# Last round of an MLP reordered, weight offsets of the squares moved, norm rows issued earlier

## The chip, the cores and the metric

The kernel runs on one core of a Trainium2 chip. The metric is the device time of one execution in microseconds (us); of several runs the median is taken, and lower is better.

## The reference

One decoder layer on 256 tokens of width 2048, all in float32:

```python
h = rms_norm(x, norm1_g); proj = h @ w_in            # q/k/v of two head groups, forget logits
y_a = fox_attention(...)                             # 8 heads, causal with forget gates
y_b = dilated_attention(...)                         # 8 heads, three dilation patterns
x = x + concat(rms_norm(y_a), rms_norm(y_b)) @ w_out
h = rms_norm(x, norm2_g)
x = x + square(relu(h @ w_mlp_in)) @ w_mlp_out       # 2048 -> 8192 -> 2048
return rms_norm(x, final_norm_g)
```

## The kernel before

**Products.** Every float32 product is made of three matmuls. Each operand is split into an upper part (rounded to the format that TensorE takes, by ScalarE) and the rest (VectorE): `whi`, `wlo` for weights, `aT_hi`, `aT_lo` for activations; upper x upper, upper x lower and lower x upper are added up in PSUM. So TensorE needs, for each 256 rows of a weight chunk (a step), one ScalarE pass and one VectorE pass over the raw weights, which SP's queue loads a megabyte at a time into four `raw` tiles.

**Chunks and steps.** A chunk is 512 columns of a weight matrix. The 12 projection chunks and 8 output chunks come first, then the MLP in four rounds r of 2048 hidden units: four up chunks u(r, c) and four down chunks d(r, c). A chunk of the MLP has 8 steps of two rows (128 inputs each). In the up chunks (`turned_product`, L414) the weights are loaded into the array and the 256 tokens are streamed: 12 matmuls of 256 columns a row, upper weights twice, then lower, for each 128 columns. In the plain down chunks (`product`, L397 to L399) the squared activations are loaded and 512 weight columns are streamed.

**Seven-product chunks.** Seven of the sixteen down chunks, d(r, 1) and d(0..2, 0), use seven block products in place of eight (`seven_products`, L457). Their sums need sums of activations, `mix_hi` and `mix_lo`, made after each up chunk from the squares, and sums of weights (`both`, made by VectorE). They come in units of four steps (near, first, odd, even), woven into other chunks by `mixed`: d(r, 0) into the up chunks of the next round, d(r, 1) together with the plain d(r, 2). They hold the four PSUM banks `sc`, `sc`, `tr`, `tr`; plain chunks use the four `acc` banks. `drain_seven` empties the four banks into `xs` in four parts after the chunk's last unit, on VectorE, with two copies by ScalarE.

**Order.** It is written out by hand in `steps`. A round is: four up chunks (with the d of the round before woven in), then the plain d(r, 3), then the pair of d(r, 1) and d(r, 2). The last round leaves d(3, 3) for the end, so there it is: up chunks with d(2, 0) woven in, the pair, the plain d(3, 0), and d(3, 3) in `last_chunk`. Beside each row of a step, `run_side` issues what was put there with `at(slot, ...)`; there are two slots a step. All engines work in program order, so what stands behind a waiting instruction on its engine waits too.

**End.** `last_chunk` goes through the first 128 tokens at full width, then the other 128 tokens in two halves of 256 columns, so that `finish` (norm, gain, scaling, output DMAs) of the first runs under the products of the second. The final gain row `gf`, 1 MB spread over all partitions, is loaded by `load_gf` on SP's queue once the `late` pool is given up, whose place in memory it takes; `copies` of `drain_seven` lies in that pool. `put_gain` multiplies a 512-column piece by it on VectorE.

**Offsets.** Tiles are laid out so that operands start at chosen offsets within lines of 64 elements (256 bytes): `NEAR` = 8, `HIGH` = 24, `LOW` = 56, `MIX_HI` = 24, `MIX_LO` = 24 + 32. The pool `wide` starts with an 8-element tile `ahead`, so `aT_hi`, `aT_lo`, `big_hi` and `big_lo`, each 4096 elements a partition, all start at 8. `big_hi` and `big_lo` hold the attention's output first and then, in all four rounds, the squares. Weights of up chunks lie at 24 (upper) and 56 (lower); those of down chunks, which are streamed, at 8.

**Norm rows.** Near the start, `first_norm_rows` (slot 22) makes a diagonal of the norm factors on VectorE (L579), one matmul that spreads it over the partitions (L580), and a copy by ScalarE, which the drains of q and k chunks use.

Of the kernel before, what the change touches and what calls it, by code (L numbers as in the profile page):

```python
# [11 lines left out]
F32 = mybir.dt.float32  # L12
# [7 lines left out]
P = 128  # L20
# [4 lines left out]
NH = 8  # L25
# [16 lines left out]

LINE, NEAR, HIGH, LOW, GATED = 64, 8, 24, 56, 48
MIX_HI, MIX_LO = 24, 32
TURNED = "qku"
WARM, WARM2 = 8, 3

# [27 lines left out]
def kernel(  # L75
# [32 lines left out]
    dram = ctx.enter_context(tc.tile_pool(name="dram", bufs=1, space=DRAM))  # L108
    attention = ExitStack()
    mix = attention.enter_context(tc.tile_pool(name="mix", bufs=1))  # L110
    mix.tile([P, 40], F32, name="mix_begin")
    ctx.enter_context(tc.manual_schedule())


# [33 lines left out]
    for r in range(ROUNDS):  # L148
        for c in range(4):
            mine = plain(index["u", (r, c)])  # L150
            steps += mine[:4] + (mixed(index["d", (r - 1, 0)], c, mine[4:]) if r else mine[4:])
        late = [index["d", (r, c)] for c in range(4)]
        if r < ROUNDS - 1:
            steps += plain(late[3])
        for unit in range(4):
            steps += mixed(late[1], unit, plain(late[2])[2 * unit:2 * unit + 2])
        if r == ROUNDS - 1:
            steps += plain(late[0]) + plain(late[3])

    last_slot = {chunks[ci][:2]: 2 * i + 1 for i, (ci, _, _) in enumerate(steps)}  # L160
    units = list(dict.fromkeys((ci, s // 2) for ci, s, _ in steps))
# [224 lines left out]
    def operands(what, key):  # L386
        if what == "o":
            return yT_hi, yT_lo, key[0] * NH
        if what == "d":
            return hT_hi, hT_lo, 0  # L390
        return aT_hi, aT_lo, 0

    def product(acc, a, kt, t, w, j, cols, go, end):

        (ah, al, base), (hi, lo) = a, w
        xh, xl = (p[:, base + kt, t * P:(t + 1) * P] for p in (ah, al))
        nc.tensor.matmul(acc, xh, hi[:, j, cols], start=go, stop=False, skip_group_check=True)  # L397
        nc.tensor.matmul(acc, xl, hi[:, j, cols], start=False, stop=False, skip_group_check=True)  # L398
        nc.tensor.matmul(acc, xh, lo[:, j, cols], start=False, stop=end, skip_group_check=True)  # L399

    def turned_product(ci, i, j, kt, kts):

# [15 lines left out]
    def products(i, j):  # L418
        ci, s, sub = steps[i]
        what, key, _, _, _, cols, kts = chunks[ci]  # L420
        if sub:
            return seven_products(i, j)
        kt = 2 * s + j
        if what in TURNED:
            return turned_product(ci, i, j, kt, kts)
        a = operands(what, key)
        if cols > CW:
            return gated_products(ci, i, j, kt, kts, a)
        if kt == 0:
            accs[ci] = [psum.tile([P, CW], F32, name="acc", bufs=4) for _ in range(TB)]  # L430
        go, end = kt == 0, kt == kts - 1
        for t in range(TB):
            product(accs[ci][t], a, kt, t, splits[i], j, slice(0, CW), go, end)

    def seven_products(i, j):

        ci, s, sub = steps[i]
        if ci not in accs:
            accs[ci] = [psum.tile([P, CW], F32, name=n) for n in ("sc", "sc", "tr", "tr")]
        one_, two_, three, four = accs[ci]  # L440
        half, k1, k2 = CW // 2, 2 * s + j, 2 * s + 2 + j
        lower, upper = slice(0, P), slice(P, SEQ)
        h, m = (hT_hi, hT_lo), (mix_hi, mix_lo)
        todo = {
            "near": ((one_, 0, h, k2, lower), (one_, half, m, k2, lower)),
            "first": ((three, 0, h, k1, lower),),
            "odd": ((two_, half, m, k2, upper), (four, 0, m, k1, upper)),
            "even": ((three, half, m, k1, lower), (two_, 0, h, k2, upper)),
        }[sub]
        begin = j == 0 and s == 0  # L450
        hi, lo = splits[i]
        for n, (bank, c0, (ah, al), k, tokens) in enumerate(todo):
            acc = bank[:, c0:c0 + half]
            fresh = begin and (bank, sub) in ((one_, "near"), (three, "first"), (two_, "odd"), (four, "odd")) and (
                bank is not one_ or n == 0)
            for x, (a, w) in enumerate(((ah, hi), (al, hi), (ah, lo))):
                nc.tensor.matmul(acc, a[:, k, tokens], w[:, j, n * half:(n + 1) * half], start=fresh and x == 0,  # L457
                                 stop=s == KT // 2 - 2 and j == 1 and x == 2, skip_group_check=True)

# [89 lines left out]


    qkv = {}
    yT_hi = wide.tile([P, 2 * NH, SEQ], F32R, name="big_hi")
    yT_lo = wide.tile([P, 2 * NH, SEQ], F32R, name="big_lo")

    def drain_v(g, ci):
        acc = accs.pop(ci)
# [13 lines left out]

    rows1 = mix.tile([P, SEQ], F32, name="rows1")

    def first_norm_rows():
        d = two.tile([P, CW], F32, name="nat")
        square = d[:, SEQ:SEQ + P]
        nc.gpsimd.memset(square, 1.0)
        p = psum.tile([P, 512], F32, name="tr")
        for t in range(TB):
            nc.vector.tensor_scalar(d[:, t * P:(t + 1) * P], ident, rstd1[:, t:t + 1], None, op0=ALU.mult)  # L579
        nc.tensor.matmul(p[:, :SEQ], square, d[:, :SEQ], start=True, stop=True)  # L580
        nc.scalar.activation(rows1, p[:, :SEQ], AF.Copy)

# [133 lines left out]
        rsqrt(rstd2, ssq2s, D_MODEL)  # L716
        nc.vector.tensor_tensor(rstd2sq, rstd2, rstd2, op=ALU.mult)

    hT_hi, hT_lo = yT_hi, yT_lo

    def drain_u(c, ci):


        acc = accs.pop(ci)
        kept[c] = []
        for half in range(2):
            h = two.tile([P, CW], F32, name="nat")
            nc.scalar.activation(h, acc[half], AF.Relu)
            nc.scalar.activation(h, h, AF.Square)
            k0 = 4 * c + 2 * half  # L730
            split_psum(
                hT_hi[:, k0:k0 + 2, :].rearrange("p k s -> p (k s)"),
                hT_lo[:, k0:k0 + 2, :].rearrange("p k s -> p (k s)"), h,
            )
            kept[c].append(h.rearrange("p (k s) -> p k s", k=2))
# [64 lines left out]
    def square_and_gain(t, cs, n):  # L800
        unused = two.tile([P, CW], F32, name="nat")
        nc.scalar.activation(unused[:, :cs.stop - cs.start], xs[:, t, cs], AF.Square, accum_out=ssq3[:, t, n:n + 1])
        if n not in (1, 2):
            put_gain(t, cs)

    def add_down(acc, t, cs, n):
# [65 lines left out]
    for ci, (what, key, *_rest) in enumerate(chunks[:-1]):  # L872
        e = last_slot[what, key]
        if what == "v":
            at(e, drain_v, key, ci)
            if key == 0:
                at(e + 2, forget_gates)
                at(e + 6, gate_sums)
                at(e + 4, rel_row)
                at(e + 5, rel_back)  # L880
                at(e + 55, rel_turn)
        elif what in "qk":
            for half in range(2):
                late = half if what == "k" else (2 if key else 8) + 5 * half
                at(e + late, drain_qk, key, what, ci, half)
            if what == "k":
                kind = groups[key][4]
                for h in range(4):
                    n = e + 6 + 7 * (h // 2)
                    if kind == 0:  # L890
                        at(n - 3, decay_of, groups[key][3] * 4 + h)
                    at(n, scores, key, h)
                for h in range(4):
                    at(e + 20 + 7 * (h // 2), values, key, h)
                for h in range(4):
                    at(e + 13 + 7 * (h // 2), turn_probs, key, h)
                if key % 2:
                    at(e + 33, group_norm, kind)
        elif what == "o":
            at(e, drain_o, *key, ci)  # L900
            if key[0] == 1:
                for n in range(2):
                    at(e + 2, to_features, 4 * key[1] + 2 * n, 16)
                if key[1] == 3:
                    at(e + 4, second_norm)
        elif what == "u":
            at(e, drain_u, key[1], ci)
            at(e + 2, mix_activations, key[1])
            at(e + 4, split_mixed, key[1])
        elif ci in seven:  # L910
            for part in range(4):
                at(e + 1 + 2 * part, drain_seven, *key, ci, part)
            if key[0] == ROUNDS - 1:
                at(e + 7, load_gf)
                for c in (1, 2):
                    for t in range(TB):
                        at(e + 11 + 2 * c + t, put_gain, t, slice(c * CW, (c + 1) * CW))
        else:
            at(e, drain_d, *key, ci)

# [95 lines left out]
```

## Time and profile before

| what | value |
|---|---|
| median of 3 runs | 1099.67 us (1099.06 to 1099.78) |
| the profiled execution | 1097.77 us, span 1096.0 us |
| PE busy | 1080.1 us, 99% of the span |
| VectorE (DVE) busy | 800.7 us, 73% |
| ScalarE (ACT) busy | 604.1 us, 55% |
| DMA | 209.27 MB, 191 GB/s on average |
| mean granted TensorE clock | 0.996 |

PE is TensorE's matmuls, PEld its weight loads, POOL is GpSimd, and SPq the DMA issues of SyncE. Matmuls are pipelined, so the time that one costs is the distance between starts, or a group's time in the chain divided by its count; the duration of a single record is longer. The chain is the work that ended last, followed back from the end: at each step what released it, or what stood before it on its engine. A row of a group or of the timeline gives start, duration, engine, line, operation, result<-inputs, shapes and count, and in brackets the idle time before it with what ended it. A row of the waits reads: who <- for whom: us in total, times, longest. A row of DMA issues ends with the size of one and the median time from issue to landing.

### The profile page before, as it was taken

Reading aid. Unit: us, or ns where it says so; the run is one execution under the profiler, and the core shown is the slowest. Engines: PE = TensorE matmul, PEld = TensorE weight load, DVE = VectorE, ACT = ScalarE, POOL = GpSimd, SP = SyncE. Lnnn points to the kernel's source line nnn. Section 1 sums busy time; section 2 is a strip of 40 time slices with the busy share of each in tenths; the row PEclk is TensorE's granted clock in tenths of the full one; section 3 lists DMA queues with packets and bytes.
Section 4 is the critical chain, followed back from the end, with each engine's and each line's share of the span. In section 5 each row is a group of like instructions: output and inputs, shape, how many; then the busy total and the mean of one; then the engine's idle time right before and its main releaser. Section 6 shows DMA issues by size and latency. Waiting matters only on the chain.

```text
span 1096.0 us, 19064 instructions
## 1 busy us (share of the span) xinstructions
PE 1080.1 (99%) x7877; PEld 1014.8 (93%) x7877; DVE 800.7 (73%) x1076; ACT 604.1 (55%) x821; POOL 27.9 (3%) x42
## 2 busy tenths in 40 slices
PE   9999999999999999999999999999999999998996
PEld 7999899998988899998999998999998899998886
DVE  6666756667576666578777789787778887779774
ACT  6455545546455565655546665546666556666541
POOL 0010200000001000000000000000000000000000
PEclk9999999999999999999999999999999999999999
DMA  8665464655545567646766554675665666655642
GB/s 319 235 217 169 155 200 146 193 177 170 193 154 192 165 188 224 193 158 207 216 196 199 205 203 158 206 218 187 197 212 173 194 197 186 193 196 180 215 178 77
DMA packets 105395, 209.27 MB, mean 191 GB/s; under 512 B 3971, under 2 KB 5084, under 8 KB 105180
## 3 DMA queue, kind: packets, MB, share of 16 engines
q1 hardware_dynamic: 104412, 206.59, 57.7%
q8 instruction: 61, 1.00, 0.4%
q0 software_dynamic: 304, 1.06, 0.3%
q10 hardware_dynamic: 592, 0.40, 0.1%
q14 instruction: 26, 0.21, 0.1%
HBM read 205.93 MB, written 2.11 MB: 190 GB/s over the span
## 4 chain that ended last, share of the span: by engine, by line
PE 98%; ACT 0%; DVE 0%; DMA 0%; issue 0%; POOL 0%; ACTq 0%; DVEq 0%
PE acc L414 48%; PE acc L397 11%; PE acc L398 11%; PE acc L399 11%; PE sc L457 7%; PE tr L457 5%; PE tr L349 1%; PE sc L676 1%; PE sc L632 1%; PE tr L660 0%; DMA xs<-in_x_dram 0%; PE sc L628 0%; ACT whi L252 0%; PE sc L678 0%; PE sc L398 0%
## 5 line engine op out<-in xcount | busy, mean ns | idle before, releaser
L253 DVE TENSOR_TENSOR wlo<-raw,whi 128x1024 fp32r<-128x1024 f32 (+2 forms) x327 | 394.5, 1221 | 162.0 <-ACT whi L252 161.1
L252 ACT ACTIVATE whi<-raw 128x1024 fp32r<-128x1024 f32 (+2 forms) x328 | 339.2, 1050 | 228.3 <-PE acc L414 129.9
L414 PE MATMUL acc<-aT_hi,whi 128*128 128x256 f32 x1536 | 425.6, 277 | 0.0
L414 PE MATMUL acc<-aT_hi,wlo 128*128 128x256 f32 x1536 | 424.1, 276 | 0.0
L414 PE MATMUL acc<-aT_lo,whi 128*128 128x256 f32 x1536 | 423.9, 276 | 0.0
L414 PEld LDWEIGHTS acc<-aT_hi,whi 128*128 128x128 f32 x1536 | 288.1, 188 | 1.2 <-issue 0.9
L414 PEld LDWEIGHTS acc<-aT_lo,whi 128*128 128x128 f32 x1536 | 288.2, 188 | 0.3
L414 PEld LDWEIGHTS acc<-aT_hi,wlo 128*128 128x128 f32 x1536 | 288.1, 188 | 0.1
L397 PE MATMUL acc<-whi,big_hi 128*128 128x512 f32 (+1 forms) x414 | 160.2, 387 | 0.0
L398 PE MATMUL acc<-whi,big_lo 128*128 128x512 f32 (+1 forms) x414 | 159.9, 386 | 0.0
L399 PE MATMUL acc<-wlo,big_hi 128*128 128x512 f32 (+1 forms) x414 | 159.8, 386 | 0.0
L399 PEld LDWEIGHTS acc<-wlo,big_hi 128*128 128x128 f32 x414 | 78.1, 189 | 15.8
L398 PEld LDWEIGHTS acc<-whi,big_lo 128*128 128x128 f32 x414 | 78.1, 189 | 14.4
L397 PEld LDWEIGHTS acc<-whi,big_hi 128*128 128x128 f32 x414 | 78.1, 189 | 14.2
L218 ACT ACTIVATE whi<-both 128x1024 fp32r<-128x1024 f32 x56 | 59.7, 1066 | 49.0 <-DVE both L223 17.1
L219 DVE TENSOR_TENSOR wlo<-both,whi 128x1024 fp32r<-128x1024 f32 x56 | 68.3, 1220 | 4.7 <-ACT whi L218 3.8
L336 DVE TENSOR_TENSOR big_lo<-nat,big_hi 128x512 fp32r<-128x512 f32 x32 | 22.1, 692 | 42.3 <-ACT big_hi L335 42.3
L397 PE MATMUL acc<-whi,aT_hi 128*128 128x512 f32 (+1 forms) x144 | 51.7, 359 | 0.0
L398 PE MATMUL acc<-whi,aT_lo 128*128 128x512 f32 (+1 forms) x144 | 51.0, 354 | 0.0
L399 PE MATMUL acc<-wlo,aT_hi 128*128 128x512 f32 (+1 forms) x144 | 51.0, 354 | 0.0
L218 ACT ACTIVATE whi<-raw 128x1024 fp32r<-128x1024 f32 x28 | 29.6, 1056 | 11.6 <-PE sc L457 5.0
L335 ACT ACTIVATE mix_hi<-nat 128x512 fp32r<-128x512 f32 x32 | 18.5, 625 | 29.9 <-DVE nat L745 29.9
(212 smaller groups left out, 1359.5 us busy)
## 6 DMA issues: line engine op xcount, KB each, us to landing
raw<-in_w_mlp_in_dram SPq DMA_DIRECT2D x64, 1024.0 KB, 5.6
raw<-in_w_mlp_out_dram SPq DMA_DIRECT2D x64, 1024.0 KB, 5.1
raw<-in_w_in_dram SPq DMA_DIRECT2D x42, 1024.0 KB, 5.2
raw<-in_w_out_dram SPq DMA_DIRECT2D x16, 1024.0 KB, 5.1
raw<-in_w_in_dram SPq DMA_DIRECT2D x4, 1040.0 KB, 9.5
xs<-in_x_dram SPq DMA_DIRECT2D x3, 512.0 KB, 9.5
raw<-in_w_in_dram SPq DMA_DIRECT2D x2, 512.0 KB, 5.3
big_lo<-rel_d POOLq DMA_DIRECT2D x1, 1024.0 KB, 7.1
```

The costliest lines, as they stand in the source:

```text
L218: nc.scalar.activation(hi, src, AF.Copy)
L219: nc.vector.tensor_tensor(lo, src, hi.bitcast(F32), op=ALU.subtract)
L252: nc.scalar.activation(hi[:, :, c:c + step], t[:, :, c:c + step], AF.Copy)
L253: nc.vector.tensor_tensor(lo, t, hi.bitcast(F32), op=ALU.subtract)
L335: nc.scalar.activation(hi, src, AF.Copy)
L336: nc.vector.tensor_tensor(lo, src, hi.bitcast(F32), op=ALU.subtract)
L349: nc.tensor.transpose(p[:, j * SEQ + t * P:j * SEQ + (t + 1) * P], xs[:, t, c:c + P], ident)
L397: nc.tensor.matmul(acc, xh, hi[:, j, cols], start=go, stop=False, skip_group_check=True)
L398: nc.tensor.matmul(acc, xl, hi[:, j, cols], start=False, stop=False, skip_group_check=True)
L399: nc.tensor.matmul(acc, xh, lo[:, j, cols], start=False, stop=end, skip_group_check=True)
L414: nc.tensor.matmul(acc, w[:, j, b * P:(b + 1) * P], a[:, kt, :], start=kt == 0 and b % 2 == 0 and n == 0, stop=kt == kts - 1 and n == 2, s ...
L457: nc.tensor.matmul(acc, a[:, k, tokens], w[:, j, n * half:(n + 1) * half], start=fresh and x == 0, stop=s == KT // 2 - 2 and j == 1 and x ...
```

## The change

1. In the last round the plain chunk d(3, 0) moves ahead of the pair d(3, 1) and d(3, 2). The pair is then followed by `last_chunk`. The gain products of chunks 0, 1 and 2 are all issued at the end of the last chunk's first pass, chunk 0's too, which came with its squares before.
2. The three matmuls of a seven-product term come as upper x upper, upper x lower, lower x upper, so that the squares' upper part is loaded twice in a row (`seven_products`).
3. `big_lo` and `big_hi` change places and get 48 and 32 elements more. In rounds 0 and 1 the squares lie at 24 (upper) and 56 (lower) within the lines, in rounds 2 and 3 at 8 as before, as the attention's output does. The plain down chunks of rounds 0 and 1 also load the upper part twice in a row.
4. The diagonal of `first_norm_rows` is made at slot 19 by a function of its own; the matmul and the copy stay at slot 22.
5. Two pads shrink from 40 to 24 elements, which keeps the other pools' offsets.

```diff
+BIG_HI, BIG_LO, SHIFTED = 32, 48, 2
...
-    mix.tile([P, 40], F32, name="mix_begin")
+    mix.tile([P, 24], F32, name="mix_begin")
...
-        if r < ROUNDS - 1:
-            steps += plain(late[3])
+        steps += plain(late[3 if r < ROUNDS - 1 else 0])
         for unit in range(4):
             steps += mixed(late[1], unit, plain(late[2])[2 * unit:2 * unit + 2])
         if r == ROUNDS - 1:
-            steps += plain(late[0]) + plain(late[3])
+            steps += plain(late[3])
...
         if what == "d":
-            return hT_hi, hT_lo, 0
+            return *squares_of(key[0]), 0
...
-    def product(acc, a, kt, t, w, j, cols, go, end):
+    def product(acc, a, kt, t, w, j, cols, go, end, turn=False):
...
         nc.tensor.matmul(acc, xh, hi[:, j, cols], start=go, stop=False, skip_group_check=True)
-        nc.tensor.matmul(acc, xl, hi[:, j, cols], start=False, stop=False, skip_group_check=True)
-        nc.tensor.matmul(acc, xh, lo[:, j, cols], start=False, stop=end, skip_group_check=True)
+        rest = ((xl, hi), (xh, lo))
+        for n, (x, part) in enumerate(rest[::-1] if turn else rest):
+            nc.tensor.matmul(acc, x, part[:, j, cols], start=False, stop=end and n == 1, skip_group_check=True)
...
-            product(accs[ci][t], a, kt, t, splits[i], j, slice(0, CW), go, end)
+            product(accs[ci][t], a, kt, t, splits[i], j, slice(0, CW), go, end, what == "d" and key[0] < SHIFTED)
...
-            for x, (a, w) in enumerate(((ah, hi), (al, hi), (ah, lo))):
+            for x, (a, w) in enumerate(((ah, hi), (ah, lo), (al, hi))):
...
-    yT_hi = wide.tile([P, 2 * NH, SEQ], F32R, name="big_hi")
-    yT_lo = wide.tile([P, 2 * NH, SEQ], F32R, name="big_lo")
+    big_lo = wide.tile([P, KT * SEQ + BIG_LO], F32R, name="big_lo")
+    big_hi = wide.tile([P, KT * SEQ + BIG_HI], F32R, name="big_hi")
+
+    def rows_at(big, at):
+        return big[:, at:at + KT * SEQ].rearrange("p (k s) -> p k s", k=KT)
+
+    yT_hi, yT_lo = rows_at(big_hi, BIG_HI - 16), rows_at(big_lo, 0)
...
+    def first_norm_diagonal():
         d = two.tile([P, CW], F32, name="nat")
-        square = d[:, SEQ:SEQ + P]
-        nc.gpsimd.memset(square, 1.0)
-        p = psum.tile([P, 512], F32, name="tr")
+        diagonal.append(d)
+        nc.gpsimd.memset(d[:, SEQ:SEQ + P], 1.0)
         for t in range(TB):
             nc.vector.tensor_scalar(d[:, t * P:(t + 1) * P], ident, rstd1[:, t:t + 1], None, op0=ALU.mult)
...
+    def squares_of(r):
+        return (rows_at(big_hi, BIG_HI), rows_at(big_lo, BIG_LO)) if r < SHIFTED else (yT_hi, yT_lo)
...
-        if n not in (1, 2):
+        if n > 2:
             put_gain(t, cs)
...
                 at(e + 7, load_gf)
-                for c in (1, 2):
+                for c in range(3):
                     for t in range(TB):
-                        at(e + 11 + 2 * c + t, put_gain, t, slice(c * CW, (c + 1) * CW))
+                        at(e + 16 + c, put_gain, t, slice(c * CW, (c + 1) * CW))
...
+    at(19, first_norm_diagonal)
     at(22, first_norm_rows)
...
-            late5.tile([P, 40], F32R, name="late_begin")
+            late5.tile([P, 24], F32R, name="late_begin")
```

More of the change, by code (lines that the diff above doesn't have):

```diff
@@ L442, in seven_products @@
         lower, upper = slice(0, P), slice(P, SEQ)
-        h, m = (hT_hi, hT_lo), (mix_hi, mix_lo)
+        h, m = squares_of(chunks[ci][1][0]), (mix_hi, mix_lo)
         todo = {
@@ L571, with first_norm_rows @@
     rows1 = mix.tile([P, SEQ], F32, name="rows1")
-    def first_norm_rows():
+    diagonal = []
+    def first_norm_diagonal():
         d = two.tile([P, CW], F32, name="nat")
-        square = d[:, SEQ:SEQ + P]
-        nc.gpsimd.memset(square, 1.0)
-        p = psum.tile([P, 512], F32, name="tr")
+        diagonal.append(d)
+        nc.gpsimd.memset(d[:, SEQ:SEQ + P], 1.0)
         for t in range(TB):
             nc.vector.tensor_scalar(d[:, t * P:(t + 1) * P], ident, rstd1[:, t:t + 1], None, op0=ALU.mult)
+    def first_norm_rows():
+        d = diagonal.pop()
+        square = d[:, SEQ:SEQ + P]
+        p = psum.tile([P, 512], F32, name="tr")
         nc.tensor.matmul(p[:, :SEQ], square, d[:, :SEQ], start=True, stop=True)
@@ L717, in second_norm, with drain_u @@
         nc.vector.tensor_tensor(rstd2sq, rstd2, rstd2, op=ALU.mult)
-    hT_hi, hT_lo = yT_hi, yT_lo
-    def drain_u(c, ci):
+    def squares_of(r):
+        return (rows_at(big_hi, BIG_HI), rows_at(big_lo, BIG_LO)) if r < SHIFTED else (yT_hi, yT_lo)
+    def drain_u(r, c, ci):
+        hT_hi, hT_lo = squares_of(r)
         acc = accs.pop(ci)
@@ L906 @@
         elif what == "u":
-            at(e, drain_u, key[1], ci)
+            at(e, drain_u, *key, ci)
             at(e + 2, mix_activations, key[1])
```

## The prediction

> **What bounds the kernel now.** I read the engine line and the chain's shares first, then the chain piece by piece around the down projections, then the waits, then the timeline of VectorE and of the queue SP at the two places where TensorE stands still, and at the end.
>
> ```profile
> span 1096.0 us, 19064 instructions
> PE 1080.1 (99%) x7877; PEld 1014.8 (93%) x7877; DVE 800.7 (73%) x1076; ACT 604.1 (55%) x821; POOL 27.9 (3%) x42
> PE 98%; ACT 0%; DVE 0%; DMA 0%; issue 0%; POOL 0%; ACTq 0%; DVEq 0%
> ```
>
> TensorE carries 98% of the chain, and the other engines have room on average. So time can come from three things only: the spacing of matmuls, places where TensorE waits, and the tail after the last matmul. All sums are made against the profiled execution (1097.77 us, of which 1096.0 is the span); the median of the runs shown is 1099.67, 1.9 above it, and I take the savings off that median. A change of about 0.2%, 2.2 us, is the least that a measurement of this kernel tells from none.
>
> Spacing, from the chain in order of time (start, duration, what):
>
> ```profile
> 546.02 0.23 PE acc L397
> 546.70 10.90 PE acc L414 x96
> 557.60 1.43 PE sc L457 x12
> 559.03 0.71 PE tr L457 x6
> ```
>
> An up-projection matmul (L414, 256 columns) takes 10.90/96 = 0.1135 us. A matmul of a seven-product term (L457), also 256 columns, takes 1.43/12 = 0.119 or 0.71/6 = 0.118: 5 ns more. A seven-product chunk has 4 units x 2 rows x 7 products x 3 terms = 168 such matmuls, so it loses 0.85 us; there are seven such chunks.
>
> **Part 1, the plain chunk ahead of the pair.** Today the last round goes straight from the end of chunk d(2,0) into d(3,1), which wants the same four banks.
>
> ```profile
> PE tr L457 <- DVE xs L777: 3.3, 1, 3.3
> 998.72 0.69 DVE L336 TENSOR_TENSOR big_lo<-nat,big_hi 128x512 fp32r<-128x512 f32 x1 [0.53 <-ACT big_hi L335]
> 1000.81 0.74 DVE L777 SCALAR_TENSOR_TENSOR xs<-tr,rstd2sq,xs 128x512 f32<-128x512 f32 x1
> 1001.61 0.70 PE tr L457 x3
> 1001.60:1004.70 3.10, 3.09 (x13) 2.81 (x14) 3.00 (x6) 1.86 (x4) 0.00 (x0) 0.56 0.77 253
> 1004.70:1008.00 3.30, 3.30 (x18) 2.86 (x17) 3.30 (x5) 1.80 (x2) 0.00 (x0) 0.89 0.21 80
> ```
>
> TensorE waits 3.3 us for the drain of the last bank (L777, over at 1001.55), which stands on VectorE behind the split of fresh squares. Then the clock is lower: the two last rows (stretch, busy time of PE, PEld, DVE, ACT and POOL, then the granted clock) show 0.56 over 3.10 us and 0.89 over 3.30, a loss of 3.10 x 0.44 + 3.30 x 0.11 = 1.7 us. With some 0.2 us of issue time around the wait (an estimate) the place costs 5.2 us. After the change eight plain steps of 12 matmuls at 0.227 (546.02 to 546.70 is three), 21.8 us, stand between the two users of the banks; the earlier rounds have this order already and no wait there comes near the list's top. So -5.2, whole: d(3,0) uses other banks (acc), and its drain lies under the pair.
>
> What is late next is the end. The gain row `gf` lies where the `late` tiles were, so its DMA waits on SP until `copies` has been read in part 2 of the drain of d(3,1). Today that falls into d(3,0), with the whole last chunk still to come; now it falls into the last chunk itself, and all six whole-width gain products (two per chunk c = 0, 1, 2) stand behind it on VectorE, ahead of the last chunk's own drain.
>
> ```profile
> 1042.71 0.39 PE L397 MATMUL acc<-whi,big_hi 128*128 128x512 f32 x1
> 1051.77 0.42 DVE L792 TENSOR_TENSOR tr<-tr,copies 128x256 f32<-128x256 f32 x1
> 1052.35 0.45 SPq L760 DMA_DIRECT2D gf<-in_final_norm_g_dram  x1
> 1062.12 2.50 DVE L820 TENSOR_TENSOR xs<-xs,gf 128x512 f32<-128x512 f32 x4
> 1064.47 0.39 PE L397 MATMUL acc<-aT_hi,big_hi 128*128 128x512 f32 x1
> 1073.77 0.15 DVE L824 TENSOR_REDUCE ssq3s<-ssq 128x1 f32<-128x3 f32 x1
> 1075.55 0.75 DVE L808 SCALAR_TENSOR_TENSOR xs<-acc,rstd2sq,xs 128x512 f32<-128x512 f32 x1 [1.45 <-PE acc L399]
> 1078.77 1.46 DVE L843 TENSOR_SCALAR xs<-xs,rstd,fi_u 128x384 f32<-128x384 f32 x3
> 1081.31 0.48 DVE L808 SCALAR_TENSOR_TENSOR xs<-acc,rstd2sq,xs 128x256 f32<-128x256 f32 x1 [1.07 <-PE acc L399]
> 1082.95 0.15 DVE L825 TENSOR_SCALAR ssq3s<-ssq3s 128x1 f32<-128x1 f32 x1
> 1087.06 0.48 DVE L808 SCALAR_TENSOR_TENSOR xs<-acc,rstd2sq,xs 128x256 f32<-128x256 f32 x1 [3.96 <-PE acc L399]
> raw<-in_w_mlp_out_dram SPq DMA_DIRECT2D x64, 1024.0 KB, 5.1
> out_dram<-xs SPq DMA_DIRECT2D x2, 320.0 KB, 2.8
> xs<-in_x_dram SPq DMA_DIRECT2D x3, 512.0 KB, 9.5
> ```
>
> The chunk behind the pair starts at 1042.71, and gf is issued 9.6 us later (1052.35). Let L be the start of the last chunk, 1064.47 today. The two splits and the drain parts around it come in the same order after the change, so gf goes out at about L + 9.6. A megabyte lands after 5.1 us: L + 14.7. Then on VectorE: six gain products at 2.50/4 each, 3.75; the sum of squares, 0.3; the block from 1075.55 to 1080.23 (drain and scaling of the first token half), 4.7; the block from 1081.31 to 1083.10, 1.8. That ends at L + 25.3. Today the last drain starts at 1087.06 = L + 22.6. So the tail slips by 2.7 us at this landing time; with the 2.8 us of the 320 KB transfer by 0.4, with the 9.5 us of the crowded first loads by 7.1. SP has no weights left to load then, so I lean a little to the short side: +2.4. The products' number does not change, nor do the squares.
>
> **Part 2, norm rows sooner.**
>
> ```profile
> 39.12 0.29 DVE L870 CAST gcat<-nat 128x256 fp32r<-128x256 f32 x1
> 43.10 1.24 DVE L253 TENSOR_TENSOR wlo<-raw,whi 128x1040 fp32r<-128x1040 f32 x1 [1.94 <-ACT whi L252]
> 44.27 0.47 DVE L579 TENSOR_SCALAR nat<-ident,rstd 128x128 f32<-128x128 f32 x2
> 44.89 0.67 PE L580 MATMUL tr<-nat 128*128 128x256 f32 x2 [1.35 <-DVE nat L579]
> 35.61 0.22 POOL L576 MEMSET nat<- 128x128 f32 x1
> ```
>
> The diagonal (two tensor_scalar, 0.47 us) stands behind the split that ends at 44.3, and TensorE waits 1.35 us for it. At slot 19 it stands right behind the gcat copy and is done at about 39.9; the split behind it slips by 0.5 us at most, with a step in hand. POOL's memset ran at 35.61 already and keeps its place between the same neighbours. -1.35; bounds 0 (if the next weight split becomes the wait) and 1.5 (with the issue time around it).
>
> **Part 3, offsets and order.** Moving operands of the down chunks sit at 8 elements (mod 64), the squares at 8 (both parts), the mixed parts at 24 and 56, as the up-projection's weights do. Single matmuls at the end of an up step:
>
> ```profile
> 563.61 0.28 PE L414 MATMUL acc<-aT_hi,wlo 128*128 128x256 f32 x1
> 563.72 0.28 PE L457 MATMUL tr<-whi,mix_hi 128*128 128x256 f32 x1
> 563.83 0.28 PE L457 MATMUL tr<-whi,mix_lo 128*128 128x256 f32 x1
> 563.95 0.28 PE L457 MATMUL tr<-wlo,mix_hi 128*128 128x256 f32 x1
> 564.06 0.28 PE L457 MATMUL sc<-whi,big_hi 128*128 128x256 f32 x1
> 564.18 0.28 PE L457 MATMUL sc<-whi,big_lo 128*128 128x256 f32 x1
> 508.14 0.40 PE L397 MATMUL acc<-whi,big_hi 128*128 128x512 f32 x1
> 508.85 0.39 PE L397 MATMUL acc<-whi,big_hi 128*128 128x512 f32 x1
> ```
>
> The first mixed product keeps the pace of the up step (0.11 a matmul); with the squares at 8 it goes to 0.12 and stays there. In rounds 0 and 1 the squares now sit at 24 and 56 and the order upper, upper, lower is that of L414: the whole sequence of offsets is that of the up step, which holds 0.1135 for 96 matmuls on end. So the four seven-product chunks that read them (d(0,0), d(0,1), d(1,0), d(1,1)) should lose their excess: -4 x 0.85 = -3.4. In rounds 2 and 3 (three chunks, 2.5 us of excess) the squares stay at 8, and the mixed products have the same cycle of offsets as before, only started elsewhere: 0, with bounds of -1.4 (all of the mixed products' share, 8 of 14) and +1.4. The plain chunks of rounds 0 and 1 (4 x 96 = 384 matmuls) have run at 0.227 when settled; in the three after a seven-product term it is 0.71/3 = 0.237 (508.14 to 508.85). No row shows 512 columns with weights at 24 and 56. Bounds: -0.3 (eight such places in the two rounds, three or four matmuls each, no longer unsettled) and +384 x 0.010 = +3.8. I take -0.3, by the up step, whose offsets these are.
>
> Here the Trainium skill speaks against the change. TensorE: Matmul & The Clock Gate, Part 2, on what each phase is for, says that the weight load has a read port of its own and takes nothing from the running matmul; by that, offsets and order are worth nothing, and the sum is 1095.5 instead of 1091.8 (rival B). The rows from 563.72 to 564.18, with equal shapes and two paces, do not agree with it; no run here takes the offsets alone away yet.
>
> The larger tiles only move neighbours by 256 bytes; the pads are cut so that every other offset stays. The new rows of round 2 overlap old ones by 16 and 48 elements, always rows already read: 0.
>
> **Sum.** -5.2 + 2.4 - 1.35 - 3.4 - 0.3 = -7.85: 1099.67 - 7.85 = 1091.8.
>
> **Rivals.**
> A, the forecast, 1091.8; its own range is 1089.5 to 1094.
> B, the offsets do nothing and the order neither: the excess belongs to the terms' change of banks and weights, whatever the offsets. For it: it is alike on squares and mixed parts (0.118 to 0.119); against it: the three matmuls from 563.72 on. -5.2 + 2.4 - 1.35 = -4.15: 1095.5.
> C, the tail does not slip, because gf goes out or lands sooner (2.8 us), and the rest comes as summed: -7.85 - 2.4 + 0.4 = -9.85: 1089.8; with the mixed products of the later rounds at the up pace 1088.4.
> D, the seven-product terms gain, but 512 columns at 24/56 stay at the unsettled pace: -7.85 + 0.3 + 3.8 = -3.75: 1095.9; without the gain -4.15 + 3.8 = -0.35: 1099.3, no change.
> E, slower: the pace is a state that the up step falls out of and regains (lost in the terms before 546.02, it held for the 96 matmuls from 546.70 on). If with the new offsets it is not regained in rounds 0 and 1, their 1536 up matmuls lose 5 ns each, 7.7 us, beside the 3.8 of D, with no gain of part 3: -4.15 + 7.7 + 3.8 = +7.35: 1107.0. It decides once these losses pass 4.15 + 2.2 = 6.35 us, some 80% of the up matmuls or a third of them with all of D. Against it: the up step regained the pace after every kind of neighbour so far.
>
> **Chances.** A 0.50, B 0.17, C 0.14, D 0.13 (0.08 with the gain, 0.05 without), E 0.06. The range 1088.0 to 1096.5 leaves out E, D without the gain and the outer end of C, together some 0.15. Faster by over 0.2% are A, B, C and the first D: 0.89, less 0.03 for a slip of the tail near its far bound in B: 0.86. Same: D without the gain and that slip: 0.08. Slower: 0.06.
>
> **What would show it.** No wait of TensorE on L777's line near the start of the last pair, and a granted clock of 1.0 through the last round. The wait for the diagonal gone. Groups of twelve seven-product matmuls at 1.36 us in the chain for the chunks of rounds 0 and 1, still 1.42 in rounds 2 and 3. At the end, gain products that start only with gf's landing, and a last drain that waits for VectorE's queue, not for TensorE. Wrong would make it: weight splits too late for the first pass of the last chunk, which takes a step every 1.36 us; plain chunks at more than 0.227; or a tail that finds gf landed in time.

## The result, and the profile after

| | median of the runs | range | ratio to before (95%) |
|---|---|---|---|
| before, same chip | 1099.37 us | 1098.77 to 1099.78 | |
| changed kernel | 1089.97 us | 1089.07 to 1092.41 | 0.9921 [0.9905, 0.9937] |

The gain between the medians is 9.4 us; by the ratio it is 0.8%, with an interval of 6.9 to 10.4 us. The forecast was 7.85 (1091.8), inside that interval. The profiled execution of the changed kernel took 1089.07 us, 8.7 less than that of before. Lines have moved: up matmuls are L415, plain ones L397 and L400, seven-product ones L458, the gain products L833, the drains of plain and last chunks L821.

The head of the page, and the chain's shares:

```profile
span 1087.3 us, 18969 instructions
PE 1074.9 (99%) x7877; PEld 1009.4 (93%) x7877; DVE 800.2 (74%) x1076; ACT 604.3 (56%) x821; POOL 27.9 (3%) x42
PE 95%; DVE 2%; DMA 1%; ACT 0%; issue 0%; POOL 0%; ACTq 0%; DVEq 0%; SPq 0%
```

VectorE (2%) and a DMA (1%) have entered a chain that was 98% TensorE: a new tail. TensorE's waits, then stretches of the last round (length, TensorE's busy time, granted clock, DMA):

```profile
PE tr L349 <- DMA xs<-in_x_dram: 1.4, 1, 1.4
PE sc L316 <- DVE relx L293: 1.2, 1, 1.2
```

```profile
995.00:1000.00 5.00, 5.00 (x24) 1.00 0.13 48
1010.00:1015.00 5.00, 5.00 (x31) 1.00 0.62 210
```

Both large waits of before, for the bank and for the diagonal, are gone from the list; what is left lies at the very start. The plain chunk runs through 990 to 1012 at full clock and the pair begins behind it without a gap. The chain at a seven-product chunk woven into up steps (round 0), at one in a pair (round 1), and in round 3:

```profile
545.48 10.93 PE acc L415 x96
556.41 1.36 PE sc L458 x12
557.77 0.68 PE tr L458 x6
694.66 1.41 PE sc L458 x12
696.07 0.68 PE tr L458 x6
1023.85 1.40 PE sc L458 x12
1025.25 0.72 PE tr L458 x6
```

Twelve in 1.36 us is the pace of the up step; the woven chunks of rounds 0 and 1 have it throughout, the pair only for the six in 0.68. In round 3, forecast to stay at 1.42 and 0.71, the twelve take 1.40.

The norm rows, on VectorE and TensorE:

```profile
39.58 0.47 DVE L586 TENSOR_SCALAR nat<-ident,rstd 128x128 f32<-128x128 f32 x2
43.62 0.59 PE L592 MATMUL tr<-nat 128*128 128x256 f32 x2
```

The diagonal is ready at 40.05, 3.6 us ahead of its products. The end of the chain, in order of time, and then the timeline of TensorE and VectorE from the start of the last chunk:

```profile
1063.56 4.64 DMA gf<-in_final_norm_g_dram
1068.22 3.70 DVE xs L833 x6
```

```profile
1054.86 0.39 PE L397 MATMUL acc<-aT_hi,big_hi 128*128 128x512 f32 x1
1063.04 0.42 DVE L805 TENSOR_TENSOR tr<-tr,copies 128x256 f32<-128x256 f32 x1
1068.22 3.70 DVE L833 TENSOR_TENSOR xs<-xs,gf 128x512 f32<-128x512 f32 x6 [3.33 <-DMA gf<-in_final_norm_g_dram]
...
1077.14 0.28 PE L400 MATMUL acc<-wlo,big_hi 128*128 128x256 f32 x1
1078.38 0.48 DVE L821 SCALAR_TENSOR_TENSOR xs<-acc,rstd2sq,xs 128x256 f32<-128x256 f32 x1
```

VectorE sits idle for 3.33 us until gf lands, and the last drain starts 1.24 us after the start of the last matmul with no wait shown for TensorE: it stands in VectorE's own queue. Before the change that distance was 0.32 us.

To compare spacing I add up, from the starts of the matmuls in a trace, what each takes until the next one starts beyond 0.1133 us (256 columns) or 0.2267 (512), the best sustained pace here; other widths count in proportion. These sums are called excess below; TensorE's waits are in them. They are given without the first 60 matmuls, whose start is treated further down: 28.3 us before, 18.45 after.

### The profile page after: what moved, and what is told of

It is laid out like the page before. It is cut to its first block, busy times and chain, and to the rows that moved or that the text cites. A ratio compares the mean times of both kernels' runs of the same rounds, so it can differ in the third digit from the quotient of the medians.

```text
span 1087.3 us, 18969 instructions
## 1 busy us (share of the span) xinstructions
PE 1074.9 (99%) x7877; PEld 1009.4 (93%) x7877; DVE 800.2 (74%) x1076; ACT 604.3 (56%) x821; POOL 27.9 (3%) x42
## 4 chain that ended last, share of the span: by engine, by line
PE 95%; DVE 2%; DMA 1%; ACT 0%; issue 0%; POOL 0%; ACTq 0%; DVEq 0%; SPq 0%
PE acc L415 48%; PE acc L400 21%; PE acc L397 11%; PE sc L458 7%; PE tr L458 5%; PE tr L349 1%; PE sc L688 1%; PE sc L644 1%; DVE wlo L253 1%; PE tr L672 0%; DMA xs<-in_x_dram 0%; DMA gf<-in_final_norm_g_dram 0%; DVE xs L833 0%; PE sc L400 0%; ACT whi L252 0%
## 5 line engine op out<-in xcount | busy, mean ns | idle before, releaser
L415 PE MATMUL acc<-aT_hi,whi 128*128 128x256 f32 x1536 | 425.6, 277 | 0.0
L415 PE MATMUL acc<-aT_hi,wlo 128*128 128x256 f32 x1536 | 424.0, 276 | 0.0
L415 PE MATMUL acc<-aT_lo,whi 128*128 128x256 f32 x1536 | 423.8, 276 | 0.0
L415 PEld LDWEIGHTS acc<-aT_hi,whi 128*128 128x128 f32 x1536 | 288.2, 188 | 1.2 <-issue 0.9
L415 PEld LDWEIGHTS acc<-aT_lo,whi 128*128 128x128 f32 x1536 | 288.2, 188 | 0.3
L415 PEld LDWEIGHTS acc<-aT_hi,wlo 128*128 128x128 f32 x1536 | 288.1, 188 | 0.0
L397 PE MATMUL acc<-whi,big_hi 128*128 128x512 f32 (+1 forms) x414 | 160.3, 387 | 0.0
L400 PE MATMUL acc<-whi,big_lo 128*128 128x512 f32 (+1 forms) x414 | 160.2, 387 | 0.0
L400 PE MATMUL acc<-wlo,big_hi 128*128 128x512 f32 (+1 forms) x414 | 159.5, 385 | 0.0
L400 PEld LDWEIGHTS acc<-wlo,big_hi 128*128 128x128 f32 x414 | 77.8, 188 | 15.8
L400 PEld LDWEIGHTS acc<-whi,big_lo 128*128 128x128 f32 x414 | 77.9, 188 | 15.0
L397 PEld LDWEIGHTS acc<-whi,big_hi 128*128 128x128 f32 x414 | 77.9, 188 | 14.2
L397 PE MATMUL acc<-whi,aT_hi 128*128 128x512 f32 (+1 forms) x144 | 51.7, 359 | 0.0
L400 PE MATMUL acc<-whi,aT_lo 128*128 128x512 f32 (+1 forms) x144 | 51.0, 354 | 0.0
L400 PE MATMUL acc<-wlo,aT_hi 128*128 128x512 f32 (+1 forms) x144 | 51.0, 354 | 0.0
L335 ACT ACTIVATE mix_hi<-nat 128x512 fp32r<-128x512 f32 x32 | 18.5, 625 | 29.9 <-DVE nat L758 29.9
```

Of the source, the lines that this page charges most:

```text
L335: nc.scalar.activation(hi, src, AF.Copy)
L400: nc.tensor.matmul(acc, x, part[:, j, cols], start=False, stop=end and n == 1, skip_group_check=True)
L415: nc.tensor.matmul(acc, w[:, j, b * P:(b + 1) * P], a[:, kt, :], start=kt == 0 and b % 2 == 0 and n == 0, stop=kt == kts - 1 and n == 2, s ...
```

## The experiments

Twelve kernels were run, all variants of the changed one, in three groups, each on a chip of its own: the early gf and the first three on offsets and order; then gf twice, two more on order and the better version; then the four on each part undone. In these groups the kernel before had medians of 1098.84, 1099.15 and 1099.06 us, so medians of different groups compare to some 0.5 us.

**The tail: gf early, and gf twice.** The first takes the memory of gf from the raw tile that the last chunk's first weights give up, so that its load need not wait for the drain.

```diff
-        late_forms.close()
-        gf = late_tiles["gf"] = ctx.enter_context(tc.tile_pool(name="gain", bufs=1)).tile(...)
+        gf = wraw.tile([P, 4, CW + NH], F32, name="raw").rearrange("p k c -> p (k c)")[:, :D_MODEL]
+        late_tiles["gf"] = gf
...
-                at(e + 7, load_gf)
+                at(e + 1, load_gf)
+                at(e + 7, late_forms.close)
```

> The changed kernel, but the gain row is loaded into the raw tile that the last chunk's first weights give up, some 8 us sooner. Theory (the end hangs on gf's landing: gain products idle 3.33 us for it, last drain at 1078.38 against a last matmul that ends near 1077.1): the slip goes, 1.2 to 1.3 us off the profiled span (1087.3 to about 1086.1), the median falls by 1 to 2 us and the runs lie closer together, since the landing time no longer reaches the end. Rival (the end is bound by VectorE's queue itself, gf or not): within 0.3 us of the changed kernel and the same spread.

Measured: 1088.5 us (1087.82 to 1089.5), ratio 0.9902 [0.9887, 0.9917], which does not part from the changed kernel's by its interval. The trace does, on SP's queue and VectorE:

```profile
1050.70 0.34 SPq L773 DMA_DIRECT2D raw<-in_final_norm_g_dram  x1
1066.40 3.69 DVE L833 TENSOR_TENSOR xs<-xs,raw 128x512 f32<-128x512 f32 x6
1079.03 0.48 DVE L821 SCALAR_TENSOR_TENSOR xs<-acc,rstd2sq,xs 128x256 f32<-128x256 f32 x1 [2.39 <-PE acc L400]
```

The products wait for nothing and the last drain waits for TensorE again. It starts 0.32 us after the start of the last matmul (1078.71), as before the change, so the tail is 0.9 us shorter. The runs did not draw together as expected: they still lie in groups 1.3 to 1.7 us apart, so gf's landing is not what spreads them.

The second issues gf's transfer twice.

```diff
-        nc.sync.dma_start(
+        for _ in range(2): nc.sync.dma_start(
             gf, ...
```

> The changed kernel with the transfer of the gain row issued twice into the same tile (1 MB more at the end, nothing else). Theory (the tail hangs on the landing: gf, then the gain products on VectorE, then the last drain): the second copy lands some 4.3 us later (one copy takes 4.64, less what the two share), the products and the last drain move by all of it: about +4.3, 1094.3. Rival (the tail is set by VectorE's queue whatever gf does, or by TensorE): under +1: below 1091.

Measured: 1094.11 us (1093.36 to 1094.95), +4.1. VectorE:

```profile
1073.96 3.70 DVE L833 TENSOR_TENSOR xs<-xs,gf 128x512 f32<-128x512 f32 x6 [7.92 <-DMA gf<-in_final_norm_g_dram]
1084.13 0.47 DVE L821 SCALAR_TENSOR_TENSOR xs<-acc,rstd2sq,xs 128x256 f32<-128x256 f32 x1
```

The idle time before the products goes from 3.33 to 7.92, by 4.6 us. The last drain now starts 5.84 us after the start of the last matmul (1078.29) in place of 1.24, so the end takes all of it; the medians differ by 4.1. With the run before, this shows the tail: the landing of gf sets the end of the changed kernel.

**Offsets and order.** Five runs vary them. First, squares at 24 and 56 in all four rounds.

```diff
-BIG_HI, BIG_LO, SHIFTED = 32, 48, 2
+BIG_HI, BIG_LO, SHIFTED = 32, 48, 4
```

> The squares at 24 and 56 in all four rounds (SHIFTED 4). Theory (what the offsets give the seven-product chunks they take from the plain chunks): in rounds 2 and 3 the woven chunk goes from 0.58 to 0 us over the up pace and the chunks of the pair from 0.56 to 0.38, but the two plain chunks of a round go from 0.24 to 0.94 together: about the same time, within 0.5 us of the changed kernel. Rival, as forecast (offsets give each chunk its whole excess and cost the plain chunks nothing): 1.7 to 2 us faster than the changed kernel.

Measured: 1090.95 us (1089.15 to 1091.34), ratio 0.9922 [0.9909, 0.9934]: the same as the changed kernel. The pair of round 2 now reads as those of rounds 0 and 1:

```profile
843.85 1.38 PE sc L458 x12
845.23 0.68 PE tr L458 x6
```

The seven-product chunks of the later rounds gain 0.9 us together, and the plain chunks lose more: 0.50 and 0.44 us of excess in each of four rounds, against 0.03 and 0.21 with the squares at 8, and 0.25 in the wide pass of the last chunk, which had none. The balance lies in the two narrow passes of the last chunk. Their 96 matmuls of 256 columns have 0.63 us of excess with the squares at 8, before the change too, and none at 24 and 56. Total excess is 18.7 against 18.45.

Second, the squares at 24 and 56 in rounds 0 and 1 and the plain chunks in their old order.

```diff
-            product(accs[ci][t], a, kt, t, splits[i], j, slice(0, CW), go, end, what == "d" and key[0] < SHIFTED)
+            product(accs[ci][t], a, kt, t, splits[i], j, slice(0, CW), go, end)
```

> The plain chunks of rounds 0 and 1 in the old order (upper, lower, upper loaded) at the new offsets. Theory one (the offsets cost the plain chunks 0.47 us and 0.14 us over before, whatever the order): plain chunks unchanged at 0.50 and 0.44, time within 0.3 us. Theory two (loading the same part twice in a row costs them): back to 0.03 and 0.3, 1.2 us less than the changed kernel.

Measured: 1088.97 us (1088.08 to 1090.73), ratio 0.991 [0.9897, 0.9924]. The plain chunks keep their excess (0.49 and 0.47), so it is the offsets that cost them, not the order of their terms. The pairs of rounds 0 and 1 gain, 0.38 to 0.20 each, with 1.38 us in the groups of twelve, and the total falls to 18.1:

```profile
696.20 1.38 PE sc L458 x12
697.58 0.68 PE tr L458 x6
```

Third, the squares at 8 in all rounds, with the new order of terms.

```diff
-BIG_HI, BIG_LO, SHIFTED = 32, 48, 2
+BIG_HI, BIG_LO, SHIFTED = 32, 48, 0
```

> The squares at 8 in all rounds (SHIFTED 0), order of the terms as changed. Theory (offsets and order each have a part, and the plain chunks pay for the offsets): all seven-product chunks at about 0.57 us over the up pace as rounds 2 and 3 show, 1.5 us lost there, 1.2 to 1.4 us won back in the plain chunks, 0.2 us lost in up steps: within 0.5 us of the changed kernel. Rival as forecast (order nothing, offsets all): 3.7 us slower than the changed kernel.

Measured: 1089.16 us (1088.67 to 1090.4), ratio 0.9912 [0.9898, 0.9925]: no loss, with an excess of 18.5 against 18.45. The woven chunk of round 0 and the pair of round 1:

```profile
557.37 1.41 PE sc L458 x12
558.78 0.72 PE tr L458 x6
695.73 1.40 PE sc L458 x12
697.13 0.72 PE tr L458 x6
```

Seven-product chunks lie at 0.56 to 0.58 in every round, between 0.85 before and 0 to 0.38 with the offsets. I took this to mean that the order matters first and the offsets only help it. Two runs tested that. The first takes the old order of the seven-product terms with the new offsets (the plain chunks of rounds 0 and 1 keep their new order):

```diff
-            for x, (a, w) in enumerate(((ah, hi), (ah, lo), (al, hi))):
+            for x, (a, w) in enumerate(((ah, hi), (al, hi), (ah, lo))):
```

> The changed kernel with one thing undone: the seven-product terms go back to upper, lower, upper; the new offsets and the order of the plain chunks stay. Theory (order first: loading the same upper part twice in a row is what lets TensorE hold the pace, the offsets only help it): the pair's groups of twelve go back to 1.42 us in all rounds, the seven chunks' loss back to about 0.85 us each, from 0.38, 0, 0.38, 0, 0.56, 0.58 and 0.56, so +3.5 us: about 1093.4. Rival (the offsets carry rounds 0 and 1, as the prediction had it): only rounds 2 and 3 fall back, +0.85 us: about 1090.8, with woven groups of rounds 0 and 1 still at 1.36.

Measured: 1089.76 us (1089.75 to 1090.93). Woven chunk of round 0, pair of round 1, pair of round 3:

```profile
556.35 1.36 PE sc L458 x12
557.71 0.68 PE tr L458 x6
694.52 1.38 PE sc L458 x12
695.90 0.68 PE tr L458 x6
1024.50 1.42 PE sc L458 x12
1025.92 0.71 PE tr L458 x6
```

My theory fell. In rounds 0 and 1 the old order keeps the pace even better than the new one (0.17 and 0 a chunk), and only where the squares are at 8 it falls back to 0.85. Excess rises by 0.8, to 19.2, the rival's number.

The second turns the terms of the up-projection to upper, lower, upper:

```diff
-        terms = ((hi, aT_hi), (hi, aT_lo), (lo, aT_hi))
+        terms = ((hi, aT_hi), (lo, aT_hi), (hi, aT_lo)) if chunks[ci][0] == "u" else (...)
```

> The changed kernel with the up-projection's terms turned to upper, lower, upper (the weights' upper part no longer loaded twice in a row); offsets, chunks and work stay. Theory (order first): its 3072 matmuls leave 0.1135 us for about 0.118, the groups of 96 in the chain go from 10.93 to 11.4, and the time rises by up to 3072 x 0.005 = 15 us: about 1104, and by 7 at the least. Rival (the cycle of the offsets 24 and 56 alone keeps the pace, in whatever order): 0, 1090. Second rival (one order is as good as the other where nothing else breaks the pace; only after a break does the order matter): 1 to 4 us.

Measured: 1090.33 us (1088.62 to 1090.49), no change. The groups of 96, at 24 and 56, hold 0.1135:

```profile
547.31 10.90 PE acc L415 x96
558.21 1.36 PE sc L458 x12
```

So loading the same part twice in a row is not what keeps the pace there.

**Each part undone.** The three runs that each undo one part start from a base whose runs lie closer together, the changed kernel with eleven products ahead of the first x instead of eight; more on its start follows below.

```diff
-WARM, WARM2 = 8, 3
+WARM, WARM2 = 11, 3
```

> The changed kernel with eleven products instead of eight ahead of the first x, and nothing else: the quiet base for the three runs beside it. Theory (the late start comes of TensorE's idle stretch before x): all runs within 0.5 us of each other, at 1088.8 to 1089.2 (the best version's 1087.45 plus the 1.2 and 0.4 of the two edits that are left out here). Rival (one of those two edits did it): runs from 1089 to 1091 as before.

Measured: 1089.01 us (1088.7 to 1089.23), as expected.

Part 1 undone:

```diff
-        steps += plain(late[3 if r < ROUNDS - 1 else 0])
+        if r < ROUNDS - 1:
+            steps += plain(late[3])
...
-            steps += plain(late[3])
+            steps += plain(late[0]) + plain(late[3])
...
-        if n > 2:
+        if n not in (1, 2):
...
-                for c in range(3):
+                for c in (1, 2):
...
-                        at(e + 16 + c, put_gain, t, slice(c * CW, (c + 1) * CW))
+                        at(e + 11 + 2 * c + t, put_gain, t, slice(c * CW, (c + 1) * CW))
```

> The base with part 1 alone undone: the last pair straight behind d(2,0), d(3,0) after it, the gain products at their old places. Theory: TensorE loses the 4.4 us of the bank wait and the 0.9 of the half clock again, and the last drain waits for TensorE again, 0.9 less: +4.4 on the base, about 1093.4. Rival (the tail gave back the 2.4 of the prediction): +2.9, about 1091.9.

Measured: 1093.64 us (1091.78 to 1094.35), +4.6 on the base. The wait, the granted clock behind it (it follows the busy time and count of a stretch), and the last drain:

```profile
PE tr L459 <- DVE xs L791: 3.2, 1, 3.2
```

```profile
997.00:999.00 2.00, 1.62 (x11) 0.92 0.44 135
999.00:1001.00 2.00, 2.00 (x6) 0.50 0.96 372
1001.00:1003.00 2.00, 2.00 (x8) 0.73 0.05 17
```

```profile
1082.61 0.48 DVE L822 SCALAR_TENSOR_TENSOR xs<-acc,rstd2sq,xs 128x256 f32<-128x256 f32 x1 [3.95 <-PE acc L401]
```

The bank wait and the half clock are back, 5.5 us of excess together (23.9), and the tail has no slip. Four runs of this kernel spread over 2.6 us, those of the base over 0.5; the two sets do not overlap.

Part 3 undone:

```diff
-BIG_HI, BIG_LO, SHIFTED = 32, 48, 2
+BIG_HI, BIG_LO, SHIFTED = 32, 48, 0
...
-            for x, (a, w) in enumerate(((ah, hi), (ah, lo), (al, hi))):
+            for x, (a, w) in enumerate(((ah, hi), (al, hi), (ah, lo))):
```

> The base with part 3 undone whole: squares at 8 in every round, upper, lower, upper in the seven-product terms, plain chunks in the old order. Theory (from the spacing in the traces): seven chunks at 0.85 instead of 2.5 in all, +3.4; the up steps around them +0.5; the plain chunks of rounds 0 and 1 -1.1: +2.8 on the base, about 1091.8. Rival one, the prediction's terms (3.4 + 0.3, nothing lost in the plain chunks): +3.7. Rival two, by which neither offsets nor order matter: 0.

Measured: 1091.64 us (1091.44 to 1091.72), +2.6 on the base; the excess is 21.4, +3.0. The woven chunk of round 0:

```profile
556.07 1.43 PE sc L458 x12
557.50 0.71 PE tr L458 x6
```

Part 2 undone:

```diff
-    at(19, first_norm_diagonal)
+    at(22, first_norm_diagonal)
     at(22, first_norm_rows)
```

> The base with part 2 undone: the diagonal is built at slot 22 again, right ahead of its products. Theory: TensorE waits for it again, +1.6 (the prediction had 1.35). Rival (the saved wait had come back as waits for weight splits a little later): under +0.5.

Measured: 1090.46 us (1090.37 to 1090.69), +1.45, with the wait back:

```profile
PE tr L592 <- DVE nat L586: 1.4, 1, 1.4
```

**A better version**, from three findings: gf early, plain chunks in the old order, eleven products at the start.

```diff
-WARM, WARM2 = 8, 3
+WARM, WARM2 = 11, 3
...
-            product(accs[ci][t], a, kt, t, splits[i], j, slice(0, CW), go, end, what == "d" and key[0] < SHIFTED)
+            product(accs[ci][t], a, kt, t, splits[i], j, slice(0, CW), go, end)
... (and gf early as above)
```

> Three edits on the changed kernel: the gain row loaded early (as in the run with gf early), the plain chunks of rounds 0 and 1 in their old order, and eleven products instead of eight ahead of the first x (they fill TensorE's idle stretch from 5.0 to 6.3 us). Theory: -1.2 and -0.4 from the first two; the clock rises about 4 us after the first product in every run, not about 9 us after it in some, so that the runs that start late (1.7 us more) go away: 1087.6 to 1088.0, all runs within 0.5 us of each other. Rival (the late start hangs on something else than the idle stretch): runs still in two groups 1.7 us apart. Second rival (the added products hold up the first transposes): about 0.4 more.

Measured: 1087.45 us (1087.36 to 1087.54), ratio 0.9892 [0.9877, 0.9907]: 2.5 us under the changed kernel, and all runs within 0.2 us. Of that, eleven products alone gave 1.0 by the medians, and the other two edits some 1.6 more.

## Why the prediction was right, and where its terms were off

| step | forecast | traces, before to after | that part undone |
|---|---|---|---|
| part 1, bank wait and clock | -5.2 | -5.3 | |
| part 1, tail slip | +2.4 | +0.9 | |
| part 1 together | -2.8 | -4.4 | -4.6 |
| norm rows | -1.35 | -1.6 | -1.45 |
| offsets and order, settling | -3.7 | -2.9 | -2.6 |
| sum | -7.85 | -8.9 | -8.7 |

The traces' sum is the excess and the tail; it stands beside 8.7 us between the two profiled executions, since the changed one lost 0.25 at the start. The norm rows' 1.6 lies just past the bound of 1.5.

**Part 1** came as worked out: the wait on the bank's drain, the lower clock behind it, and nothing late in their place until the end.

**The tail** is the term that was mis-sized most; its mechanism was right. With L = 1054.86, gf was issued at L + 8.7 (forecast 9.6), took 4.64 (5.1, the median of the weight loads), and the products started at L + 13.4 (14.7). From there the working held: 3.70 for the products, the first drain at 1072.10, the last at L + 23.5. Against L + 22.6 before, that is 0.9. Why gf went out sooner than in the chunk it was read from, no run here takes apart. A slip that is the difference of two long chains, 25.3 and 22.6, takes every error of either whole. It is the largest of the errors: -1.5 us here, -0.35 in part 1's wait and the norm rows, +0.8 in the offsets. Together they make the 1.05 between the forecast and the traces' sum; the other 0.5 of the gain of the medians is not in the two traces.

**Offsets and order.** The forecast of -3.4 for the four chunks of rounds 0 and 1 measured -2.6: the two woven ones gained all 0.85, those in the pairs 0.47 each. In the pairs a plain step stands between the units: right behind it twelve terms take 1.41 us, and only the later ones are back at the pace of 0.68 for six. Taking later rounds as unchanged was wrong by 0.8 in their chunks (0.85 to 0.56 or 0.58 each, by the order), and the up steps of rounds 1 to 3 gained another 0.5. The -0.3 for the plain chunks of rounds 0 and 1 had the wrong sign: they lost 1.2, from 0.03 and 0.29 a round to 0.50 and 0.44, while those of rounds 2 and 3 gained 0.2. That is rival D in small (its price was 3.8): 512 columns with the squares at 24 and 56 have that excess in every run that has them there, in either order. So these terms come within 0.8 us of the forecast partly by luck: gains that were put at nothing cancel a loss that was put at a gain.

The runs fill this square (excess of one seven-product chunk, pair and woven, by the order of its terms):

| | upper, lower, upper | upper, upper, lower |
|---|---|---|
| squares at 8 | 0.85, 0.84 | 0.56, 0.58 |
| squares at 24 and 56 | 0.17, 0 | 0.38, 0 |

In the lower row the plain chunks beside the pair have their new order; in their old order, the pair's 0.38 is 0.20. The offsets were the right reason for the woven chunks and most of the pairs' gain in rounds 0 and 1; the order of a chunk's own terms helps only where the squares are at 8. Net on the whole kernel, the excess falls from 21.4 (both old) to 19.2 by the offsets with the old order in the seven-product terms, to 18.5 by the order alone, and to 18.45 by both, since the offsets' gain is partly handed back by the plain chunks. So the order alone, which the forecast put at nothing, is worth as much as the whole of part 3. The offsets with both old orders, in the plain chunks too, were not run.

**Rival B**, by which neither matters, falls with part 3 undone: +2.6 us. The place alone shows in the woven chunk of round 0, with the old order of terms in both runs: twelve equal matmuls take 1.43 us with the squares at 8 and 1.36 at 24 and 56, 5% less. The Trainium skill (TensorE: Matmul & The Clock Gate, Part 2, on what each phase is for) says that loading the next weights takes no read bandwidth from the running matmul. What the prediction drew from this, that offsets are worth nothing, these rows do not bear out. Whether the load holds up the matmul or is slower itself, no run here shows.

**Rival C** (gf out or landed sooner, a slip of only 0.4, 1089.8) was nearer than the forecast in the tail: gf went out 0.9 us sooner and took 0.5 less, and the slip was 0.9. Its time is also the measured one within 0.2 us, but that is partly luck, since it stands on a sum of -9.85 where the traces have -8.9. The early gf takes the rest of the slip away. **Rival E** did not happen: in the chain, every group of 66 or more up matmuls of the MLP takes 0.1133 to 0.1140 us each, in every variant, even with their own terms turned.

## What to carry to other kernels

When work is moved toward the end of a kernel, price the transfer that its buffer's release sets off, and look for memory that comes free earlier; here an earlier place for gf took away the whole 0.9 us by which the tail had slipped. When a spacing of matmuls is to be improved by placing operands, count every kind of matmul that reads them: the plain 512-column chunks gave back 1.2 of the 2.6 us that the seven-product chunks of the same rounds won. Undo each part on a base whose runs agree to a few tenths before crediting parts with 1 or 2 us.

## What the runs showed of the hardware

**Two starts.** Runs of several of these kernels fell into groups over 1 us apart. The first matmuls of the variant with all squares at 8 (late start), then of the better version:

```profile
4.56 0.42 PE L349 MATMUL tr<-ident,xs 128*128 128x128 f32 x1
6.26 0.90 PE L349 MATMUL tr<-ident,xs 128*128 128x128 f32 x3 [1.27 <-DMA xs<-in_x_dram]
7.88 1.42 PE L415 MATMUL acc<-aT_hi,whi 128*128 128x256 f32 x4
```

```profile
1.18 4.65 PE L316 MATMUL sc<-nat 128*128 128x512 bf16 x11 [1.18 <-DVE relx L293]
6.17 0.55 PE L349 MATMUL tr<-ident,xs 128*128 128x128 f32 x3 [0.23 <-DMA xs<-in_x_dram]
7.17 0.71 PE L415 MATMUL acc<-aT_hi,whi 128*128 128x256 f32 x4
```

Four equal matmuls take 1.42 us in one and 0.71 in the other: TensorE is still at half pace at 7.88. In the profiled executions with eight products ahead of x, the first 30 matmuls had an excess of 3.9 to 4.3 us, or of 5.3 to 6.0. The wait for x leaves TensorE idle for 1.1 to 1.7 us in there. With three more products in that stretch 0.2 to 0.9 us of it are left, and the runs of the four kernels without the bank wait spread over 0.5, 0.3, 0.3 and 0.2 us. The length of the wait alone does not sort the starts: an early one had 1.71 us, a late one 1.15. The Trainium skill (TensorE: Matmul & The Clock Gate, Part 1) says that the clock rises after a busy window of about 3.4 us, and that the window runs free of the kernel's start; the two groups agree with that, since half pace ends about 4 us after the first product in the better version and about 9 us after it in the other, behind the wait, though no run here shows the window itself. The granted clock in the profile reads 1.0 through this start, so only the spacing shows it.

**A stall and the spread.** With the bank wait in and eleven products at the start, four runs spread over 2.6 us; without it over 0.2 to 0.5. In the one with a trace the clock behind the wait read 0.50 for 2 us. That a stall spreads the runs is not shown by this: the kernel before has the same wait, and in one group eight of its nine runs lie within 0.3 us (1098.65 to 1098.95). It also has eight products at the start, so why it does not fall into two groups stays open.

**Pace is a state.** The same matmul takes 0.113 or 0.118 to 0.119 us depending on what ran before it. In the changed kernel's pairs of rounds 0 and 1, six matmuls run at 0.68/6 = 0.113 directly behind twelve at 1.41/12 = 0.1175, with the same offsets and shapes. What sets and clears this state is not settled by these runs beyond the square above.
